# One gathered block's weighted sum of rows moved from VectorE to TensorE, by diagonal matmuls, in a hybrid decoder block

## The chip, the cores and the metric

The kernel runs on one core of one Trainium2 chip. The metric is the device time of one execution in microseconds (us); smaller is better. TensorE (PE) multiplies matrices, VectorE (DVE) and ScalarE (ACT) work element by element, GpSimd (POOL) here issues the gathers and does some subtractions, SyncE (SP) issues the other DMAs.

## The reference

A decoder block on 1024 tokens of width 1024: windowed attention and a gated short convolution (the mixer), a layer norm, and then a channel mixer in which each token uses 128 of 16384 experts (8 heads with 16 each), and a second layer norm. The part that matters here:

```python
def chunk(args):
    xc, ec, gc = args                       # tokens, their 128 experts, their gates
    u = jnp.take(u_experts, ec, axis=0)
    a = jax.nn.gelu(jnp.einsum('tkd,td->tk', u, xc), approximate=False)
    vv = jnp.take(v_experts, ec, axis=0)
    return jnp.einsum('tk,tkd->td', gc * a, vv)
...
ff = peer_ffn(h, ...)
h = layer_norm(DN_ALPHA * h + ff, ln2_g[l], ln2_b[l])
```

All inputs are float32.

## The kernel before

The 1024 tokens are eight blocks of 128. Four of them (`DENSE`, blocks 2 to 5) go through all 16384 experts with dense matmuls, where a token's gate is zero for an expert that it didn't choose. The other four (`ROWS`, blocks 0, 1, 6, 7) gather their experts' rows. So TensorE and VectorE share the channel mixer.

Stage 1 (`s1`) does the mixer for groups of two blocks in order (`GROUPS`), then `normed`, then `keys_of` (16 projections "h" with float32 matmuls at L370, and the top-16 of the scores on VectorE, L196 to L200). `chosen` turns these into expert numbers (`idx`) and gates; for the dense blocks `gates_of_all` writes the gate of every expert: per eight tokens VectorE makes three masks `o1`, `oh`, `ol` (L256, L261; they share four buffers), TensorE multiplies them in two groups of four tokens (eight float16 matmuls each, L267 and L268, into the one PSUM buffer `pk`), ScalarE takes each group out with two copies into the halves of `st` (L271), and after 32 tokens two DMAs of 1 MB store both halves in memory (L275). `st` has two buffers, so the first copy of the next 32 tokens waits until these have landed.

Stage 2 (`s2`) is the dense part: `up` (L684) and `down` (L716), 6144 matmuls of 512 columns.

Beside all of this run the 1024 steps of the gathered blocks, from a generator `gathered(tb)`, in the order block 0, 1, 6, 7. For each block, 128 "u" steps: POOL gathers 128 rows of `u` (one per token, 512 KB together) with an indirect DMA (L148), and VectorE multiplies them with the tokens and sums (L150). Then 128 "v" steps: POOL gathers 128 rows of `v` (L160), and VectorE adds them, weighted per token by a column of `a`, to a PSUM accumulator (L162). Then `second_norm`. All rows, the token blocks and the norm's parameters share five buffers (tag `t4k`). POOL's queue holds the gathers in the order of the steps, and each waits for the buffer that the step five before it leaves.

Steps are drawn by `advance_rows` (beside each projection of stage 1) and by `advance` (in stage 2, spread over nine tenths of its units). A scheduler then sets the order on each engine by its own estimate of times, so steps of the first units of stage 2 stand in stage 1's last part. Each engine works in its order.

Of the kernel before, what the change touches and what calls it, by code (L numbers as in the profile page):

```python
# [13 lines left out]
F32 = mybir.dt.float32  # L14
# [5 lines left out]
AF = mybir.ActivationFunctionType  # L20
ALU = mybir.AluOpType
# [4 lines left out]
P = 128  # L26
T = 1024
D = 1024
# [7 lines left out]
ALPHA = 2.0 ** 0.25  # L36
# [5 lines left out]
GROUPS = [[0, 1], [2, 3], [4, 5], [6, 7]]  # L42
DENSE = [2, 3, 4, 5]
ROWS = [0, 1, 6, 7]
# [10 lines left out]
NGATHER = 5  # L55
# [22 lines left out]
def block_kernel(ctx: ExitStack, tc: tile.TileContext, d, out):  # L78
    nc = tc.nc
    act = nc.scalar.activation  # L80
    V = nc.vector
    G = nc.gpsimd
# [5 lines left out]
    h1d = dram.tile([NB, P, D], F32, name="h1d")  # L88
# [4 lines left out]
    ident = const.tile([P, P], F32, name="ident")  # L93
    make_identity(nc, ident)

    idx, gw, e12 = {}, {}, {}

    def layer_norm(o, src, par, small, sums=None):

        s = small.tile([P, 8], F32, name="lnst", bufs=2)  # L100
        junk = small.tile([P, D], F16, name="junk")
        if sums is None:
            act(junk, src, AF.Copy, accum_out=s[:, 0:1])
        else:
            V.tensor_reduce(s[:, 0:1], sums, axis=AX.X, op=ALU.add)  # L105
        V.tensor_scalar(s[:, 1:2], s[:, 0:1], -1.0 / D, None, op0=ALU.mult)  # L106
        act(junk, src, AF.Square, bias=s[:, 1:2], accum_out=s[:, 2:3])  # L107
        V.tensor_scalar(s[:, 3:4], s[:, 2:3], 1.0 / D, EPS, op0=ALU.mult, op1=ALU.add)  # L108
        act(s[:, 4:5], s[:, 3:4], AF.Sqrt)  # L109
        V.reciprocal(s[:, 5:6], s[:, 4:5])  # L110

        V.tensor_tensor(s[:, 6:7], s[:, 5:6], s[:, 5:6], op=ALU.mult)  # L112
        V.tensor_tensor(s[:, 6:7], s[:, 6:7], s[:, 3:4], op=ALU.mult)  # L113
        V.tensor_scalar(s[:, 6:7], s[:, 6:7], -0.5, 1.5, op0=ALU.mult, op1=ALU.add)  # L114
        V.tensor_tensor(s[:, 5:6], s[:, 5:6], s[:, 6:7], op=ALU.mult)  # L115
        V.scalar_tensor_tensor(o, src, s[:, 1:2], par[0], op0=ALU.add, op1=ALU.mult)  # L116
        V.scalar_tensor_tensor(o, o, s[:, 5:6], par[1], op0=ALU.mult, op1=ALU.add)  # L117
# [8 lines left out]
    gp = ctx.enter_context(tc.tile_pool(name="gp", bufs=1, reuse_waits="tile"))  # L126
    pg = ctx.enter_context(tc.tile_pool(name="pg", bufs=1, space=PS, reuse_waits="tile"))

    def second_norm(tb, src):
        par = []  # L130
        for i in (2, 3):
            p = gp.tile([P, D], F32, name="ln2", tag="t4k", bufs=NGATHER)
            G.dma_start(p, ln2d[:, i:i + 1].to_broadcast([P, 1, D]).rearrange("p a e -> p (a e)"))
            par.append(p)
        o = gp.tile([P, D], F32, name="o", tag="t4k", bufs=NGATHER)
        layer_norm(o, src, par, gp)
        G.dma_start(out[tb * P:(tb + 1) * P], o)

    def gathered(tb):
        g = gw[tb].rearrange("p h k -> p (h k)")  # L140
        h1 = gp.tile([P, D], F32, name="h1", tag="t4k", bufs=NGATHER)
        G.dma_start(h1, h1d[tb])
        h1p = pg.tile([P, D], F32, name="pg")
        act(h1p, h1, AF.Copy)
        a = gp.tile([P, P], F32, name="a", bufs=2)
        for k in range(P):
            row = gp.tile([P, D], F32, name="row", tag="t4k", bufs=NGATHER)
            G.indirect_dma_start(out=row, out_offset=None, in_=d["u"],  # L148
                                 in_offset=bass.IndirectOffsetOnAxis(ap=idx[tb][:, k:k + 1], axis=0))
            V.scalar_tensor_tensor(row, row, 1.0, h1p, op0=ALU.mult, op1=ALU.mult, accum_out=a[:, k:k + 1])  # L150
            yield True
        act(a, a, AF.Gelu)
        V.tensor_tensor(a, a, g, op=ALU.mult)
        acc = pg.tile([P, D], F32, name="pg")
        h1 = gp.tile([P, D], F32, name="h1", tag="t4k", bufs=NGATHER)
        G.dma_start(h1, h1d[tb])
        act(acc, h1, AF.Copy, scale=ALPHA)
        for k in range(P):
            row = gp.tile([P, D], F32, name="row", tag="t4k", bufs=NGATHER)
            G.indirect_dma_start(out=row, out_offset=None, in_=d["v"],  # L160
                                 in_offset=bass.IndirectOffsetOnAxis(ap=idx[tb][:, k:k + 1], axis=0))
            V.scalar_tensor_tensor(acc, row, a[:, k:k + 1], acc, op0=ALU.mult, op1=ALU.add)  # L162
            yield True
        second_norm(tb, acc)

    def all_gathered():
        for tb in ROWS:
            while tb not in idx:
                yield False
            yield from gathered(tb)  # L170

    steps = all_gathered()
    done = 0

    def step():
        nonlocal done
        done += bool(next(steps, False))
# [5 lines left out]
    with ExitStack() as s1:  # L183
# [304 lines left out]
        def conv(gi, c, x, y):  # L488

            blocks, nb, n, t0 = spans(gi)  # L490
            pc = project(10 + c, x, n)
            gc = p2.tile([P, NM], F32, name="cT", bufs=2)
            act(gc[:, :n], pc[:, :n], AF.Identity, bias=bias[:, 10 + c:11 + c])
            px = project(14 + c, x, n)
            u = pa.tile([P, NM + 2], F32, name="u")
            V.tensor_copy(u[:, 0:2], utail[:, c])
            V.scalar_tensor_tensor(u[:, 2:n + 2], px[:, :n], bias[:, 14 + c:15 + c], gc[:, :n],
                                   op0=ALU.add, op1=ALU.mult)
            V.tensor_copy(utail[:, c], u[:, n:n + 2])
            cv = pa.tile([P, NM], F32, name="cv")  # L500
            act(cv[:, :n], u[:, 0:n], AF.Copy, scale=convw[:, c, 0:1])
            for t in (1, 2):
                V.scalar_tensor_tensor(cv[:, :n], u[:, t:t + n], convw[:, c, t:t + 1], cv[:, :n],
                                       op0=ALU.mult, op1=ALU.add)
            pg = project(6 + c, x, n)
            V.scalar_tensor_tensor(y[:, 4 + c, :n], pg[:, :n], bias[:, 6 + c:7 + c], cv[:, :n],
                                   op0=ALU.add, op1=ALU.mult)

        def mixed(gi, y):

            blocks, nb, n, t0 = spans(gi)
            r = p1.tile([P, nb, D], F32, name="r", tag="r")
            rsum = p1.tile([P, nb, 8], F32, name="rsum", bufs=2)
            with tc.issue_after(loads[-1].ins):
                nc.sync.dma_start(r, d["x"][t0:t0 + n].rearrange("(b p) e -> p b e", p=P))
            for c in range(8):
                ps = project(18 + c, y, n)
                mT = p2.tile([P, NM], F32, name="cT", bufs=2)
                act(mT[:, :n], ps[:, :n], AF.Identity, bias=bias[:, 18 + c:19 + c])
                tp = pt.tile([P, 4, P], F32, name="tp")  # L520
                for b in range(nb):
                    nc.tensor.transpose(tp[:, b], mT[:, b * P:(b + 1) * P], ident)
                for b in range(nb):
                    rc = r[:, b, c * P:(c + 1) * P]
                    V.scalar_tensor_tensor(rc, rc, ALPHA, tp[:, b], op0=ALU.mult, op1=ALU.add,
                                           accum_out=rsum[:, b, c:c + 1])
            return r, rsum
# [41 lines left out]
        def chosen(gi):  # L569
            for tb in sorted(GROUPS[gi], key=lambda t: t in ROWS):  # L570
                yield from product_keys(tb, *best[tb])
# [34 lines left out]
        row = gb.tile([P, P], F16, name="keyrow")  # L606
# [13 lines left out]
        for scale, bits, count in ((4096.0, 7, 4), (1.0, 11, 3)):  # L620
# [3 lines left out]
            for c in _pieces(full, bits, count):  # L624
# [5 lines left out]
                        op0=ALU.is_gt, op1=ALU.mult)  # L630
# [7 lines left out]
        for gi, blocks in enumerate(GROUPS):  # L638
            x, qkv = xin
            y = p2.tile([P, NJ, NM], F32, name="y", tag="T", bufs=4)  # L640
            for b in range(2):
                a = scores(gi, b, qkv)
                conv(gi, 2 * b, x, y)
                values(b, y, *a)
                conv(gi, 2 * b + 1, x, y)
            r, rsum = mixed(gi, y)
            if gi + 1 < len(GROUPS):
                xin = rows_in(gi + 1)
            h = normed(gi, r, rsum)
            keys_of(gi, h)  # L650
            for _ in side:
                pass
            side = chosen(gi)


    with ExitStack() as s2:
# [112 lines left out]
        for i in (2, 3):  # L769
            p = gp.tile([P, D], F32, name="ln2", tag="t4k", bufs=NGATHER)  # L770
# [44 lines left out]
```

## Time and profile before

| | us |
|---|---|
| median of 3 runs | 2745.84 (2740.81 to 2745.84) |
| the profiled execution's own time | 2743.4 |
| its span in the profile | 2741.6 |
| TensorE busy in the span | 2290.9 (84%) |
| VectorE busy | 2303.3 (84%) |
| ScalarE busy | 798.1 (29%) |
| GpSimd busy | 1415.2 (52%) |

A busy TensorE is not TensorE at its peak: matmuls overlap in the records. "PEclk" is the share of TensorE's full clock (2.4 GHz) that was granted; 0.5 is its lower level (1.2 GHz). "DMA" is the mean busy share of the 16 DMA engines. Shares over the whole span are means of stages with different limits, so the stages are read apart.

### The profile page before, as it was taken

Reading aid. Unit: us, or ns where it says so; the run is one execution under the profiler, and the core shown is the slowest. Engines: PE = TensorE matmul, PEld = TensorE weight load, DVE = VectorE, ACT = ScalarE, POOL = GpSimd, SP = SyncE. Lnnn points to the kernel's source line nnn. Section 1 sums busy time; section 2 is a strip of 40 time slices with the busy share of each in tenths; the row PEclk is TensorE's granted clock in tenths of the full one; section 3 lists DMA queues with packets and bytes.
Section 4 is the critical chain, followed back from the end, with each engine's and each line's share of the span. In section 5 each row is a group of like instructions: output and inputs, shape, how many; then the busy total and the mean of one; then the engine's idle time right before and its main releaser. Section 6 shows DMA issues by size and latency. Waiting matters only on the chain. (4 is left out here: it accounts for less than half of the span.)

```text
span 2741.6 us, 33269 instructions
## 1 busy us (share of the span) xinstructions
PE 2290.9 (84%) x11032; PEld 1917.8 (70%) x11032; DVE 2303.3 (84%) x4956; ACT 798.1 (29%) x1307; POOL 1415.2 (52%) x1233
## 2 busy tenths in 40 slices
PE   8999699789887622219999999999999999999940
PEld 7888587678766522218888888888888888888830
DVE  2158889999999999978888888888888888888897
ACT  2123122242443323224232322323232332323201
POOL 1000533443353344436667676666767666666753
PEclk9899799799977755559999999999999999999975
DMA  6355999899979788899999999999999999999987
GB/s 203 99 155 175 347 376 332 311 336 354 337 286 337 253 317 293 309 337 322 343 337 340 336 352 350 341 351 335 342 354 334 347 344 346 339 342 353 335 314 263
DMA packets 293900, 862.21 MB, mean 314 GB/s; under 512 B 25824, under 2 KB 97760, under 8 KB 289504
## 3 DMA queue, kind: packets, MB, share of 16 engines
q0 software_dynamic: 150480, 548.47, 54.5%
q1 hardware_dynamic: 143248, 311.62, 33.1%
q8 instruction: 87, 1.43, 0.2%
q14 instruction: 85, 0.70, 0.1%
HBM read 815.95 MB, written 44.04 MB: 314 GB/s over the span
## 5 line engine op out<-in xcount | busy, mean ns | idle before, releaser
L148 POOL DMA_INDIRECT row<-in_u,ix x512 | 532.9, 1041 | 586.7 <-DVE row L150 242.9
L160 POOL DMA_INDIRECT row<-in_v,ix x512 | 554.8, 1084 | 474.4 <-DVE pg L162 229.9
L162 DVE SCALAR_TENSOR_TENSOR pg<-row,a,pg 128x1024 f32<-128x1024 f32 x512 | 656.4, 1282 | 33.8 <-DMA row<-in_v,ix 27.8
L684 PE MATMUL pd<-hT,uh 128*128 128x512 f32 x2048 | 635.8, 390 | 42.8 <-ACT uh L120 42.8
L150 DVE SCALAR_TENSOR_TENSOR row<-row,pg 128x1024 f32<-128x1024 f32 x512 | 611.7, 1212 | 45.4 <-DMA row<-in_u,ix 44.8
L684 PEld LDWEIGHTS pd<-hT,uh 128*128 128x128 f32 x2048 | 385.4, 188 | 123.0 <-ACT uh L120 43.0
L716 PE MATMUL pd<-Wl,vh 128*128 128x512 f32 (+1 forms) x1056 | 402.3, 383 | 0.0
L684 PE MATMUL pd<-hT,ul 128*128 128x512 f32 x1024 | 399.3, 390 | 0.0
L716 PE MATMUL pd<-Wh,vh 128*128 128x512 f32 (+1 forms) x1056 | 397.4, 383 | 0.2 <-ACT Wh L120 0.2
L716 PE MATMUL pd<-Wh,vl 128*128 128x512 f32 (+1 forms) x1056 | 392.1, 383 | 0.3 <-POOL vl L121 0.3
L121 POOL TENSOR_TENSOR vl<-vraw,vh 128x1024 fp32r<-128x1024 f32 x128 | 309.4, 2417 | 72.7 <-ACT vh L120 68.6
L267 PE MATMUL pk<-o,oh 128*128 128x128 f16 x512 | 109.2, 277 | 208.2 <-DVE oh L261 131.3
L370 PE MATMUL mm<-x,raw 128*128 128x256 f32 x1152 | 269.2, 386 | 13.1 <-DMA x<-in_xT 7.7
L120 ACT ACTIVATE vh<-vraw 128x1024 fp32r<-128x1024 f32 x128 | 135.9, 1062 | 455.7 <-PE pd L716 302.1
L722 DVE TENSOR_TENSOR accT<-accT,pd 128x512 f32<-128x512 f32 (+1 forms) x256 | 169.4, 667 | 109.8 <-PE pd L716 97.8
L370 PEld LDWEIGHTS mm<-x,raw 128*128 128x128 f32 x1152 | 215.8, 193 | 45.2 <-issue 8.1
L370 PE MATMUL mm<-h,raw 128*128 128x256 f32 x1024 | 238.1, 385 | 1.5 <-ACT h L539 1.0
L716 PEld LDWEIGHTS pd<-Wh,vl 128*128 128x128 f32 x1056 | 198.4, 188 | 39.3 <-POOL vl L121 0.7
L716 PEld LDWEIGHTS pd<-Wl,vh 128*128 128x128 f32 x1056 | 198.5, 188 | 38.9 <-DVE Wl L121 0.2
L716 PEld LDWEIGHTS pd<-Wh,vh 128*128 128x128 f32 x1056 | 198.0, 188 | 39.2 <-ACT Wh L120 0.4
L121 DVE TENSOR_TENSOR ul<-uraw,uh 128x1024 fp32r<-128x1024 f32 x128 | 159.7, 1248 | 76.1 <-ACT uh L120 70.8
L684 PEld LDWEIGHTS pd<-hT,ul 128*128 128x128 f32 x1024 | 192.8, 188 | 40.9 <-DVE ul L121 0.8
(211 smaller groups left out, 2756.0 us busy)
## 6 DMA issues: line engine op xcount, KB each, us to landing
raw<-in_wall SPq DMA_DIRECT2D x168, 512.0 KB
uraw<-in_uT SPq DMA_DIRECT2D x128, 512.0 KB
vraw<-in_vL SPq DMA_DIRECT2D x128, 512.0 KB
gd<-st SPq DMA_DIRECT2D x32, 1024.0 KB
gq<-gd SPq DMA_DIRECT2D x32, 1024.0 KB
row<-in_u,ix POOLq DMA_INDIRECT x512
row<-in_v,ix POOLq DMA_INDIRECT x512
x<-in_xT SPq DMA_DIRECT2D x16, 256.0 KB
```

Source lines behind the costliest of these rows:

```text
L120: act(dh, src, AF.Copy)
L121: eng.tensor_tensor(dl, src, dh.bitcast(F32), op=ALU.subtract)
L148: G.indirect_dma_start(out=row, out_offset=None, in_=d["u"], in_offset=bass.IndirectOffsetOnAxis(ap=idx[tb][:, k:k + 1], axis=0))
L150: V.scalar_tensor_tensor(row, row, 1.0, h1p, op0=ALU.mult, op1=ALU.mult, accum_out=a[:, k:k + 1])
L160: G.indirect_dma_start(out=row, out_offset=None, in_=d["v"], in_offset=bass.IndirectOffsetOnAxis(ap=idx[tb][:, k:k + 1], axis=0))
L162: V.scalar_tensor_tensor(acc, row, a[:, k:k + 1], acc, op0=ALU.mult, op1=ALU.add)
L267: nc.tensor.matmul(ps[:, t], oh[:, :, t2 + t], o1[:, t2 + t], start=True, stop=False)
L370: nc.tensor.matmul(ps[:, :n], w[:, j], mov[:, j, :n], start=(j == 0), stop=(j == NJ - 1))
L684: nc.tensor.matmul(ps, w[:, j], hT[z][:, j], start=(j == 0 and k == 0), stop=(j == NJ - 1 and k == 2))
L716: nc.tensor.matmul(ps, vv[:, j % 2, k], w[:, t0:t0 + n], start=(k == 0 and p == 0), stop=(k == QUAD - 1 and p == 2))
L722: V.tensor_tensor(o, o, ps, op=ALU.add)
```

## The change

The generator is taken apart: `weights_of(tb)` does a block's u steps, `summed(tb, a)` its v steps as before. Now blocks 0 and 1 do their u steps first, then block 0 does its v steps by `summed_on_pe`, then block 1 by `summed`; blocks 6 and 7 follow as before. In `summed_on_pe` ScalarE makes a 128x128 diagonal matrix `dg` with the column of `a` on its diagonal (two buffers), and TensorE multiplies it with the gathered rows, in two float32 matmuls of 512 columns that add up in PSUM over all 128 rows. The last hunk draws steps where the rest of `side` (the generator of `chosen`) is used up in the last group.

```diff
+    def weights_of(tb):
+
+        while tb not in idx:
+            yield False
         h1p = pg.tile([P, D], F32, name="pg")
-        act(h1p, h1, AF.Copy)
+        act(h1p, own(tb), AF.Copy)
         a = gp.tile([P, P], F32, name="a", bufs=2)
         for k in range(P):
...
+            row = rows_of(tb, "u", k)
             V.scalar_tensor_tensor(row, row, 1.0, h1p, op0=ALU.mult, op1=ALU.mult, accum_out=a[:, k:k + 1])
             yield True
         act(a, a, AF.Gelu)
...
+    def summed(tb, a):
+
         acc = pg.tile([P, D], F32, name="pg")
...
+        act(acc, own(tb), AF.Copy, scale=ALPHA)
         for k in range(P):
...
-            V.scalar_tensor_tensor(acc, row, a[:, k:k + 1], acc, op0=ALU.mult, op1=ALU.add)
+            V.scalar_tensor_tensor(acc, rows_of(tb, "v", k), a[:, k:k + 1], acc, op0=ALU.mult, op1=ALU.add)
             yield True
         second_norm(tb, acc)
 
+    def summed_on_pe(tb, a):
+
+        acc = pg.tile([P, D], F32, name="pg")
+        for k in range(P):
+            row = rows_of(tb, "v", k)
+            dg = gp.tile([P, P], F32, name="dg", bufs=2)
+            act(dg, ident, AF.Copy, scale=a[:, k:k + 1])
+            for z in range(0, D, 512):
+                nc.tensor.matmul(acc[:, z:z + 512], dg, row[:, z:z + 512], start=(k == 0), stop=(k == P - 1))
+            yield True
+        V.scalar_tensor_tensor(acc, own(tb), ALPHA, acc, op0=ALU.mult, op1=ALU.add)
+        second_norm(tb, acc)
+
     def all_gathered():
...
+        a0 = yield from weights_of(ROWS[0])
+        a1 = yield from weights_of(ROWS[1])
+        yield from summed_on_pe(ROWS[0], a0)
+        yield from summed(ROWS[1], a1)
+        for tb in ROWS[2:]:
+            a = yield from weights_of(tb)
+            yield from summed(tb, a)
...
             keys_of(gi, h)
             for _ in side:
-                pass
+                if gi == len(GROUPS) - 1 and done < 3 * P:
+                    step()
             side = chosen(gi)
```

Two places in the order of the built programs show where the new instructions stand. The first is TensorE's order in stage 1 after the last projection, in the gates of the last two dense blocks. Before, one group of eight matmuls (with `oh` and `ol` in turn) follows the other; here is the end of one eight-token set and the start of the next:

```order
L268 LDWEIGHTS ol
L268 MATMUL pk<-o_7424,ol 128x128
L267 LDWEIGHTS oh
L267 MATMUL pk<-o_7483,oh 128x128
L268 LDWEIGHTS ol
L268 MATMUL pk<-o_7483,ol 128x128
```

Now, at the same kind of place (line numbers are those of the changed kernel; L182 is the new matmul, L291 and L292 are the former L267 and L268):

```order
L292 LDWEIGHTS ol
L292 MATMUL pk<-o_6938,ol 128x128
L182 MATMUL pg<-row,dg 128x512 x4
L291 LDWEIGHTS oh
L291 MATMUL pk<-o_6993,oh 128x128
L292 LDWEIGHTS ol
L292 MATMUL pk<-o_6993,ol 128x128
```

So two gathered rows (four matmuls) now stand between almost every two groups of gate matmuls; behind the last score matmul of `keys_of` there are 250 of the 256 new matmuls and all 64 gate groups of these two blocks.

The second place is ScalarE's order where one set of 32 tokens ends and the next begins, with what each instruction waits for (DMAHW is the store of the former 32 tokens). Before, the copies follow each other:

```order
L271 ACTIVATE st<-pk 128x4x64 [waits PE_49]
L271 ACTIVATE st<-pk 128x4x64
L271 ACTIVATE st<-pk 128x4x64 [waits DMAHW3_49,PE_49,Activation_49]
L271 ACTIVATE st<-pk 128x4x64 [waits DMAHW4_49,Activation_49]
L271 ACTIVATE st<-pk 128x4x64 [waits PE_49]
```

Now (L180 makes a diagonal, L295 is the former L271):

```order
L295 ACTIVATE st<-pk 128x4x64 [waits PE_49]
L295 ACTIVATE st<-pk 128x4x64
L180 ACTIVATE dg<-ident,a 128x128 [waits PE_49,Activation_49] x2
L295 ACTIVATE st<-pk 128x4x64 [waits DMAHW5_49,PE_49,Activation_49]
L180 ACTIVATE dg<-ident,a 128x128 [waits PE_49,Activation_49] x2
L295 ACTIVATE st<-pk 128x4x64 [waits DMAHW6_49]
L180 ACTIVATE dg<-ident,a 128x128 [waits PE_49,Activation_49]
```

The diagonals stand in the same queue as the copies that wait for the stores, two of them ahead of the first such copy and two between the copies.

## Rows read from the trace of the kernel before

**Rows 1.** The page: the span in 40 equal slices (busy tenths, granted clock).

```profile
PE   8999699789887622219999999999999999999940
DVE  2158889999999999978888888888888888888897
PEclk9899799799977755559999999999999999999975
```

**Rows 2.** Busy time by stretch: A:B, length, then PE, PEld, DVE, ACT, POOL (instructions), PEclk, DMA share, GB/s.

```profile
548.00:847.00 299.00, 251.98 (x1457) 214.53 (x1456) 294.97 (x869) 118.12 (x246) 122.98 (x105) 0.87 0.89 325
847.00:920.00 73.00, 71.07 (x390) 61.81 (x388) 72.50 (x229) 23.04 (x46) 27.12 (x27) 0.95 0.92 341
949.00:1189.00 240.00, 66.49 (x456) 51.05 (x456) 227.70 (x604) 70.09 (x126) 113.92 (x113) 0.50 0.85 305
1189.00:1231.00 42.00, 0.34 (x1) 0.34 (x2) 24.56 (x44) 7.79 (x8) 14.14 (x15) 0.50 1.04 380
1231.00:2631.00 1400.00, 1399.47 (x6259) 1161.58 (x6259) 1191.27 (x1506) 432.01 (x539) 944.73 (x720) 1.00 0.95 341
2631.00:2715.00 84.00, 1.65 (x16) 1.41 (x13) 71.22 (x57) 0.00 (x0) 48.93 (x53) 0.53 0.95 340
```

**Rows 3.** Costliest groups of the page: the steps on VectorE, float32 matmuls and their loads.

```profile
L162 DVE SCALAR_TENSOR_TENSOR pg<-row,a,pg 128x1024 f32<-128x1024 f32 x512 | 656.4, 1282 | 33.8 <-DMA row<-in_v,ix 27.8
L150 DVE SCALAR_TENSOR_TENSOR row<-row,pg 128x1024 f32<-128x1024 f32 x512 | 611.7, 1212 | 45.4 <-DMA row<-in_u,ix 44.8
...
L370 PE MATMUL mm<-x,raw 128*128 128x256 f32 x1152 | 269.2, 386 | 13.1 <-DMA x<-in_xT 7.7
...
L370 PEld LDWEIGHTS mm<-x,raw 128*128 128x128 f32 x1152 | 215.8, 193 | 45.2 <-issue 8.1
```

**Rows 4.** Timeline of VectorE, two places: start, us, instruction.

```profile
1145.83 1.21 DVE L150 SCALAR_TENSOR_TENSOR row<-row,pg 128x1024 f32<-128x1024 f32 x1
...
1146.97 1.21 DVE L150 SCALAR_TENSOR_TENSOR row<-row,pg 128x1024 f32<-128x1024 f32 x1
...
605.26 1.27 DVE L162 SCALAR_TENSOR_TENSOR pg<-row,a,pg 128x1024 f32<-128x1024 f32 x1
606.45 0.21 DVE L205 TENSOR_TENSOR x<-x 128x128 f16<-128x128 f16 x1
```

**Rows 5.** Timeline of TensorE within the last projections.

```profile
888.44 5.35 PE L370 MATMUL mm<-h,raw 128*128 128x256 f32 x24
...
898.50 0.22 PE L267 MATMUL pk<-o,oh 128*128 128x128 f16 x1
...
898.99 1.08 PE L370 MATMUL mm<-h,raw 128*128 128x256 f32 x4
```

**Rows 6.** Timeline of ScalarE where one set of 32 tokens ends (in brackets: idle before, releaser).

```profile
1083.08 1.05 ACT L271 ACTIVATE st<-pk 128x256 f32<-128x256 f32 x2 [4.83 <-PE pk L268]
...
1085.23 1.06 ACT L271 ACTIVATE st<-pk 128x256 f32<-128x256 f32 x2 [1.10 <-issue]
...
1092.62 0.61 ACT L271 ACTIVATE st<-pk 128x256 f32<-128x256 f32 x1 [6.33 <-DMA gd<-st]
1096.15 0.60 ACT L271 ACTIVATE st<-pk 128x256 f32<-128x256 f32 x1 [2.92 <-DMA gd<-st]
```

**Rows 7.** Busy time by stretch, as in rows 2: all seven such ends, and their sum.

```profile
1048.00:1062.30 14.30, 2.67 (x12) 1.69 (x13) 14.30 (x41) 2.72 (x5) 6.21 (x6) 0.50 0.98 365
1086.30:1096.80 10.50, 1.29 (x8) 1.01 (x9) 8.79 (x23) 1.21 (x2) 4.13 (x4) 0.50 0.99 385
...
sum 80.30, PE 11.68 PEld 8.59 DVE 71.27 ACT 9.71 POOL 34.19; mean PE 1.67 PEld 1.23 DVE 10.18 ACT 1.39 POOL 4.88
```

**Rows 8.** ScalarE on a 128x128 tile: ns min/median/max, first and last start.

```profile
L152 ACT ACTIVATE a<-a x4: 309/310/310, 555.2 to 2461.8; 128x128 f32<-128x128 f32 x4
```

**Rows 9.** Busy time by stretch, as in rows 2: a pause of TensorE and what follows.

```profile
588.00:595.00 7.00, 1.84 (x19) 1.47 (x19) 7.00 (x22) 2.69 (x6) 4.72 (x3) 0.71 0.90 312
595.00:602.00 7.00, 5.11 (x32) 4.38 (x32) 7.00 (x10) 3.65 (x7) 1.14 (x1) 0.56 0.64 197
```

More of the change, by code (lines that the diff above doesn't have):

```diff
@@ L137, in second_norm, with rows_of, own @@
         G.dma_start(out[tb * P:(tb + 1) * P], o)
-    def gathered(tb):
-        g = gw[tb].rearrange("p h k -> p (h k)")
+    def rows_of(tb, table, k):
+        row = gp.tile([P, D], F32, name="row", tag="t4k", bufs=NGATHER)
+        G.indirect_dma_start(out=row, out_offset=None, in_=d[table],
+                             in_offset=bass.IndirectOffsetOnAxis(ap=idx[tb][:, k:k + 1], axis=0))
+        return row
+    def own(tb):
         h1 = gp.tile([P, D], F32, name="h1", tag="t4k", bufs=NGATHER)
         G.dma_start(h1, h1d[tb])
+        return h1
+    def weights_of(tb):
+        while tb not in idx:
+            yield False
         h1p = pg.tile([P, D], F32, name="pg")
-        act(h1p, h1, AF.Copy)
+        act(h1p, own(tb), AF.Copy)
         a = gp.tile([P, P], F32, name="a", bufs=2)
         for k in range(P):
-            row = gp.tile([P, D], F32, name="row", tag="t4k", bufs=NGATHER)
-            G.indirect_dma_start(out=row, out_offset=None, in_=d["u"],
-                                 in_offset=bass.IndirectOffsetOnAxis(ap=idx[tb][:, k:k + 1], axis=0))
+            row = rows_of(tb, "u", k)
             V.scalar_tensor_tensor(row, row, 1.0, h1p, op0=ALU.mult, op1=ALU.mult, accum_out=a[:, k:k + 1])
@@ L152, in gathered @@
         act(a, a, AF.Gelu)
-        V.tensor_tensor(a, a, g, op=ALU.mult)
+        V.tensor_tensor(a, a, gw[tb].rearrange("p h k -> p (h k)"), op=ALU.mult)
+        return a
+    def summed(tb, a):
         acc = pg.tile([P, D], F32, name="pg")
-        h1 = gp.tile([P, D], F32, name="h1", tag="t4k", bufs=NGATHER)
-        G.dma_start(h1, h1d[tb])
-        act(acc, h1, AF.Copy, scale=ALPHA)
+        act(acc, own(tb), AF.Copy, scale=ALPHA)
         for k in range(P):
-            row = gp.tile([P, D], F32, name="row", tag="t4k", bufs=NGATHER)
-            G.indirect_dma_start(out=row, out_offset=None, in_=d["v"],
-                                 in_offset=bass.IndirectOffsetOnAxis(ap=idx[tb][:, k:k + 1], axis=0))
-            V.scalar_tensor_tensor(acc, row, a[:, k:k + 1], acc, op0=ALU.mult, op1=ALU.add)
+            V.scalar_tensor_tensor(acc, rows_of(tb, "v", k), a[:, k:k + 1], acc, op0=ALU.mult, op1=ALU.add)
             yield True
         second_norm(tb, acc)
-    def all_gathered():
[L167 to L170, printed above, removed]
+    def summed_on_pe(tb, a):
[9 more added lines that the diff above has]
+        second_norm(tb, acc)
+    def all_gathered():
+        a0 = yield from weights_of(ROWS[0])
[5 more added lines that the diff above has]
+            yield from summed(tb, a)
     steps = all_gathered()
```

## The prediction

> **What bounds the kernel now.** I read the slices first [rows 1]: TensorE is nearly always busy but for a hole near the end of stage 1 and a hole at the end, and in the first hole VectorE is full. The stretches [rows 2] give each part its own limit. From 548 to 847 us VectorE is busy in 295 of 299 us: it bounds. From 847 to 920 the last 16 projections run and TensorE (71.1 of 73) and VectorE (72.5) are both full. From 920 to 1189 the gates of blocks 4 and 5 are made; in the 240 us from 949 VectorE is busy 228, TensorE 66 at the granted clock 0.50, DMA 0.85. From 1189 to 1231 both wait for loads of stage 2 (DMA 1.04 of its engines). From 1231 to 2631 TensorE is busy 1399 of 1400 us at clock 1.00 and VectorE 1191: stage 2 is TensorE's, and a later start of it is a later end. From 2631 to 2715 only v steps run, on VectorE and DMA; 27 us of norms and stores follow.
>
> So VectorE's relief can pay between 548 and 1189 and in the last 84 us, and TensorE's new work must fit into stage 1's hole.
>
> **The change, part by part.** Sums are made against the profiled execution, 2743.4 us (0.1% under the median of 2745.84).
>
> *Number of steps.* The last hunk does nothing: 84 items of `side` are left when the last group starts, and its 36 projections draw 84 (two each, and a third in 12 of them). What moves the steps is the scheduler. In the order of the built programs VectorE has, ahead of stage 2's first gate product, 389 steps before (256 u, 133 v), and now 256 u and 15 v, with TensorE's 128 beside them: 399. Between there and the last of these products 570 steps stand in both, so 55 v steps are left for the tail instead of 65. The tail's 56 steps took 84 us [rows 2], 1.5 us each: **-15 us**.
>
> *Up to the last projections: u steps instead of v steps.* Where the residual rows of the last group are done, 128 u and 90 v stood before, now 233 u; at its first top-8, 128 u and 107 v, now 256 u. Means of 1212 and 1282 ns [rows 3] overstate both, as records overlap: a u step takes 1.14 us from start to next start, a v step 1.19 [rows 4]. That is 233 x 1.14 - (146 + 107) = +13 us at the one place, and 292 - (146 + 127) = +19 us at the other. VectorE bounds there, so I take **+15 us** for the start of the projections: 847 becomes 862.
>
> *The projections* were full on TensorE already and have no u or v step on VectorE now, so their 73 us stay. They end at 935.
>
> *The gates with the new matmuls.* A float32 matmul is recorded as two: 72 projections of x with 8 matmuls each are 1152 records [rows 3]. 24 records of 256 columns take 5.35 us with 0.39 for the last one's own length, so 4.96 / 23 = 0.216 us each at the full clock [rows 5]. At 512 columns I take twice that, 0.43; a gathered row (two matmuls, four records) is 1.72 us, at half the clock 3.44. Eight gate matmuls take 0.49 us at full clock [rows 5]. After the last score matmul TensorE now has 125 rows and 64 gate groups: 125 x 1.72 + 64 x 0.49 = 215 + 31 = 246 us. The bound from below is that alone.
>
> The weight loads are taken as hidden: each of those 24 records has its own load of 0.19 us [rows 3, 5], and 0.216 has no room for it. The Trainium skill (TensorE: Matmul & The Clock Gate, Part 3, The mechanism) says that a load overlaps matmuls in flight only where it goes to other rows of the array; these loads fill all rows, so by it each would stand between two records. By that rule the sum would be an estimated 125 x 4 x 0.19 = 95 us more; the trace does not agree with it.
>
> The stores add gaps. After each 32 tokens ScalarE waits until both have landed: its next two copies came 6.3 us, and then another 2.9, late [rows 6]; the stretch from the last copy to the end of the next pair is 80.3 / 7 = 11.5 us in the mean [rows 7], with DMA at 365 to 385 GB/s, so it won't shrink. Before, VectorE worked on there. Now TensorE has the rows: it ends two rows about 2.1 us into the stretch (a copy pair ends some 1.3 us after its group), the next group at 2.6, two more rows, whose diagonals stand ahead of the wait, at 6.0. The third's diagonal comes behind the first copy, at 6.3 + 0.6 + 0.3 [rows 6, 8]: a gap of 1.2 us; it ends at 9.0, and the next group needs the second copy out of `pk`, at 11.5: 2.5 us. So 3.7 us for each of seven ends: 26 us. (Nothing, if the stores land sooner; 5.5 each, 39, if the third row waits for the second copy too.) What is late next is the row buffers, then the gathers.
>
> The clock: a pause of TensorE before 595 (1.8 of 7 us busy) is followed by a stretch at 0.56 [rows 9]. Each gap could cost nothing, or 3.5 us, if 7 us behind it run at half the clock as there. I take half of that, 1.7 each: 12 us.
>
> The last 32 tokens have five rows only; there the copies set the pace, 2.15 us per group [rows 6]: 8 x 2.15 - 5 x 1.72 - 8 x 0.49 = 5 us more, and with block 0's norm on the same queues 8. In all 246 + 26 + 12 + 8 = 292 us, where 920 to 1189 was 269: **+23 us**.
>
> *What is at nothing.* The diagonals: 128 x 0.31 us on ScalarE [rows 8], busy 70 of 240 us [rows 2]. Block 0's norm, its loads and store move from before 949 to the passage into stage 2; hidden behind stage 2's loads, at most 2 MB at 380 GB/s, 5 us. In stage 2 nothing is bound by VectorE.
>
> Sum: 15 + 23 - 15 = +23 us, **2766 us**.
>
> **Rivals.** *Faster or equal: TensorE hides the gaps.* If gaps and clock together cost less than 15 us instead of 38, the sum is zero or below; with none of them, +13 and the tail it is 13 + (254 - 269) - 15 = -17, 2726 us. For it: VectorE, the former bound, loses more than 110 steps of 1.14 us in this stretch, and TensorE had 73 us at 0.95 with hardly a gap before. Against it: the diagonals wait in ScalarE's queue behind copies that wait for DMA, and the rows fill TensorE's time already. Faster 0.21, within 0.2% 0.12.
>
> *Gathers late.* TensorE takes its rows in order, and a late one holds the gates too. The stretch moves 125 rows of 0.52 MB and 17 MB of stores, 82 MB in 292 us, 283 GB/s; before it was 305, and the ends have reached 385. Five buffers at 2.2 us a row leave 11 us for a round. But at each end a row could come 5 us late: 35 us more, 2801. Chance 0.10.
>
> *The clock stays at half.* 125 x 3.44 + 64 x 0.98 = 493 us instead of 246, 3013. At 0.50 TensorE was busy 28% of the time [rows 2]; now it would be full, and full stretches have 0.95 and more. Partly so, 0.05. *The rule on weight loads*, 2861: 0.02.
>
> **How the numbers follow.** The forecast, 2752 to 2795, has 0.50. Below: 2726 with all gaps hidden. Above: gaps of 39, clock of 25, +19, and 5 for the passage give 19 + (246 + 39 + 25 + 8 - 269) - 15 + 5 = +58, 2801, as the late gathers do. Some 0.1 lies past 2805 and 0.1 under 2726. So 2726 to 2805. A measurement of this kernel can tell 0.2%, 5.5 us, from no change: faster 0.21, same 0.12, slower 0.67.
>
> **What would show it.** The first "h" projection after 855 and the last gate copy near 1220 to 1230 instead of 1188; stage 2's first matmul some 40 us later, and stage 2 of 1400 us again; L182 with 512 records, 0.43 us apart within a row; TensorE over 80% busy in the gates at a clock over 0.8, with VectorE far from full; idle time of TensorE that ends with a diagonal or a copy, at each store; 46 v steps after TensorE's end instead of 56. I am wrong if the gates end before 1190 (gaps hidden), if rows wait for gathers or the clock for hundreds of us, or if stage 2 changes its length.

## The result, and the profile after

The changed kernel takes 2767.54 us in the median of four runs (2761.45 to 2772.54), the kernel before 2745.84 (2740.81 to 2747.0, four runs): a ratio of 1.0082 [1.0056, 1.0107], slower by 0.8%. The forecast was 2766. The profiled execution of the changed kernel is its fastest, 2761.45 us with a span of 2759.6, so against before's span of 2741.6 the traces have to explain +18 us, and the medians +22.

The page of the changed kernel, the span in 40 slices; beside [rows 1] the hole of TensorE in slices 14 to 18 is mostly filled, its clock is up there, and VectorE's 9, 9, 9, 9, 7 in these slices have become 8, 4, 4, 2, 3.

```profile
PE   8999699779876999966999999999999999999960
DVE  2158889999999844238888788888888888888898
PEclk9899799789977999987999999999999999999985
```

Busy time by stretch of the changed kernel, columns as in [rows 2]: up to the last projections, the projections, the gates, the passage, stage 2, the tail.

```profile
548.00:847.00 299.00, 243.73 (x1393) 208.30 (x1391) 295.09 (x968) 109.86 (x233) 118.91 (x117) 0.85 0.92 339
862.00:935.00 73.00, 73.00 (x425) 64.50 (x424) 62.80 (x287) 23.88 (x47) 9.07 (x9) 0.98 0.60 211
935.00:1224.00 289.00, 262.75 (x1036) 131.38 (x1034) 122.22 (x403) 130.79 (x278) 126.71 (x128) 0.98 0.83 286
1224.00:1265.00 41.00, 0.00 (x0) 0.00 (x0) 20.09 (x17) 5.96 (x7) 15.48 (x16) 0.50 1.03 369
1265.00:2665.00 1400.00, 1399.34 (x6256) 1161.71 (x6257) 1188.64 (x1506) 432.77 (x541) 926.47 (x720) 1.00 0.95 342
2665.00:2733.00 68.00, 2.01 (x19) 1.77 (x17) 58.71 (x47) 0.00 (x0) 39.84 (x44) 0.54 0.96 345
```

VectorE still bounds until the projections (295 of 299). Then the roles change over: in the gates TensorE is busy 263 of 289 us and VectorE 122, where before VectorE was full and TensorE half empty. Stage 2 is 1400 us as before; the tail has 47 instructions on VectorE where it had 57.

The groups of the gates stretch (instructions and shape | busy, mean ns | idle before, releaser) say who waits for whom now:

```profile
L182 PE MATMUL pg<-row,dg 128*128 128x512 f32 x508 | 236.6, 606 | 14.3 <-ACT dg L180 11.0 <-DMA row<-in_v,ix 3.3
...
L285 DVE TENSOR_TENSOR oh<-da,db 128x1024 f16<-128x1024 f16 x32 | 22.0, 689 | 159.7 <-PE pk L291 159.7
```

VectorE idles 159.7 us for TensorE's gate matmuls (L291), because the 508 records of 127 rows take TensorE 236.6 us. The rows themselves wait 11.0 us for diagonals and only 3.3 for gathers.

A table puts both kernels, and the experiments below, on one scale (us, read from the trace of each kernel; the five parts add up to the span): the start of the last projection; from there to the start of the last gate copy; the passage to stage 2's first matmul; stage 2 to the start of its last matmul; and the tail from there.

| kernel | to last projection | gates | passage | stage 2 | tail | span |
|---|---|---|---|---|---|---|
| before | 919.8 | 268.5 | 42.4 | 1399.9 | 111.0 | 2741.6 |
| after | 934.5 | 289.9 | 41.0 | 1399.6 | 94.6 | 2759.6 |
| order only | 936.9 | 233.4 | 42.3 | 1401.8 | 138.1 | 2752.5 |
| diagonals on VectorE | 936.5 | 300.5 | 43.0 | 1403.8 | 98.3 | 2782.1 |
| three `st` | 933.7 | 254.5 | 40.5 | 1406.2 | 120.6 | 2755.5 |
| half the rows | 937.9 | 245.6 | 45.2 | 1401.5 | 129.8 | 2760.0 |
| float32r rows | 939.6 | 213.9 | 43.7 | 1409.3 | 200.4 | 2806.9 |
| float32r, six buffers | 923.6 | 221.4 | 43.5 | 1399.4 | 104.2 | 2692.1 |
| before, six buffers | 920.1 | 272.7 | 40.1 | 1399.9 | 79.0 | 2711.8 |
| after, six buffers | 927.1 | 294.1 | 48.3 | 1398.4 | 68.4 | 2736.3 |

After against before: +14.7 up to the last projection, +21.4 in the gates, -1.4 in the passage, -0.3 in stage 2, -16.4 in the tail: +18.

### The profile page after: what moved, and what is told of

Same layout as the page of the kernel before. It is cut to its first block, busy times and chain, and to the rows that moved or that the text cites. A ratio compares the mean times of both kernels' runs of the same rounds, so it can differ in the third digit from the quotient of the medians.

```text
span 2759.6 us, 34442 instructions
## 1 busy us (share of the span) xinstructions
PE 2476.9 (90%) x11544; PEld 1992.3 (72%) x11544; DVE 2156.7 (78%) x4829; ACT 842.6 (31%) x1434; POOL 1378.8 (50%) x1233
## 5 line engine op out<-in xcount | busy, mean ns | idle before, releaser
L141 POOL DMA_INDIRECT row<-in_u,ix x512 | 526.0, 1027 | 625.0 <-DVE row L159 234.9
L141 POOL DMA_INDIRECT row<-in_v,ix x512 | 525.9, 1027 | 486.5 <-PE pg L182 199.9
L170 DVE SCALAR_TENSOR_TENSOR pg<-row,a,pg 128x1024 f32<-128x1024 f32 x384 | 493.3, 1285 | 38.4 <-DMA row<-in_v,ix 34.2
L182 PE MATMUL pg<-row,dg 128*128 128x512 f32 x512 | 238.7, 606 | 14.3 <-ACT dg L180 11.0
L394 PEld LDWEIGHTS mm<-x,raw 128*128 128x128 f32 x1152 | 216.3, 193 | 43.5 <-issue 7.9
```

The lines of the kernel that those rows point to most:

```text
L141: G.indirect_dma_start(out=row, out_offset=None, in_=d[table], in_offset=bass.IndirectOffsetOnAxis(ap=idx[tb][:, k:k + 1], axis=0))
L170: V.scalar_tensor_tensor(acc, rows_of(tb, "v", k), a[:, k:k + 1], acc, op0=ALU.mult, op1=ALU.add)
L182: nc.tensor.matmul(acc[:, z:z + 512], dg, row[:, z:z + 512], start=(k == 0), stop=(k == P - 1))
L394: nc.tensor.matmul(ps[:, :n], w[:, j], mov[:, j, :n], start=(j == 0), stop=(j == NJ - 1))
```

## The experiments

The theory, A: the float32 rows make TensorE the bound of the gates, and each row costs it more (some 1.75 us) than VectorE's step cost (1.19). Against it stood that something else sets the end of the gates: the new order of the steps, the pauses at the stores with their clock, or the gathers. The expectations, quoted below, name the theories by letters: A is this one, B says that the new order of the steps alone makes stage 2 late, and C that gathered rows come late.

**Order only.** All u steps of blocks 0 and 1 first, and every v step on VectorE:

```
-        yield from summed_on_pe(ROWS[0], a0)
+        yield from summed(ROWS[0], a0)
```

> The new order of the steps (u of blocks 0 and 1 first) with all v steps left on VectorE, no diagonal matmuls. Theory A (the loss comes from TensorE's new rows in the gates): VectorE bounds the gates again as before; the first last-group projection starts near 864 us as in the changed kernel, the last gate copy near 1190 instead of 1224, stage 2 starts near 1232; the order leaves 82 v steps to the tail instead of 65 (before) or 55 (changed), about 26 us more than before; 2755 to 2775 us in all, but by the tail, not by the gates. Theory B (the new order of the steps alone makes stage 2 late): the last gate copy stays near 1224 here too.

Measured: 2759.77 us, ratio 1.0050 [1.0033, 1.0066]. The last copy starts at 1170.3, before both kernels; the gates take 233 us, 57 less than with the matmuls. Stretches of this kernel (gates, tail):

```profile
937.00:1171.00 234.00, 78.48 (x542) 60.95 (x540) 224.61 (x558) 82.77 (x152) 118.10 (x83) 0.51 0.74 257
...
2614.00:2725.00 111.00, 2.39 (x22) 2.15 (x20) 93.38 (x74) 0.00 (x0) 65.71 (x71) 0.52 0.95 337
```

VectorE is the bound again (225 of 234), with TensorE at clock 0.51. It holds fewer steps: 84 v steps stand in this stretch, 118 u steps stood in before's. They are paid at the end, where 73 steps are left, 1.5 us each, instead of 55. The new order alone costs +17 ahead of the gates, gives 35 in them and loses 27 in the tail. So the longer gates of the changed kernel come from the matmuls and not from the order: A holds, though the gates came out shorter than expected.

The order alone is slower than before, though, by 11 us of span. Of the changed kernel's +18 only some 7 come with the matmuls: 57 us more in the gates, 44 less in the tail, where 45 steps are left instead of 73, and 6 less in the other parts. The two kernels' ratios to before, 1.0050 and 1.0082, have intervals that overlap, so these 7 us are near the edge of what the runs can tell.

**Diagonals on VectorE**, so that they don't wait behind copies in ScalarE's queue:

```
-            act(dg, ident, AF.Copy, scale=a[:, k:k + 1])
+            V.tensor_scalar(dg, ident, a[:, k:k + 1], None, op0=ALU.mult)
```

> The diagonals are made by VectorE instead of ScalarE. Theory A with its second part (the gaps at the stores come from diagonals and copies in ScalarE's queue): the gap before the third row at each of seven stores goes, the one before the copy out of the PSUM buffer stays; TensorE's idle time in the gates falls by 7 to 15 us and the last gate copy comes 5 to 15 us earlier; 2745 to 2765 us. Theory C (gathered rows come late at the stores, since DMA is full there): gaps and time unchanged within 3 us.

Measured: 2784.49 us, ratio 1.0141 [1.0125, 1.0158]: a miss. The gates became longer by 11 us, not shorter. One store end, timeline of TensorE (start, us, instruction, in brackets idle before and releaser), then three stretches across it:

```profile
1019.98 1.96 PE L182 MATMUL pg<-row,dg 128*128 128x512 f32 x4 [0.78 <-DMA row<-in_v,ix]
1024.56 0.27 PE L291 MATMUL pk<-o,oh 128*128 128x128 f16 x1 [2.62 <-ACT st L295]
...
1025.37 3.01 PE L182 MATMUL pg<-row,dg 128*128 128x512 f32 x4
```

```profile
1018.00:1024.50 6.50, 3.16 (x7) 1.01 (x6) 0.57 (x2) 1.20 (x2) 2.57 (x3) 0.97 1.01 415
1024.50:1027.50 3.00, 2.94 (x11) 1.91 (x11) 1.89 (x3) 1.14 (x3) 0.00 (x0) 0.50 0.91 373
1027.50:1058.00 30.50, 29.22 (x115) 14.50 (x115) 9.81 (x24) 6.66 (x13) 14.05 (x15) 1.00 0.77 256
```

The wait for the diagonal did go. But the gate group's wait for a copy out of `pk` (L295) remains, and here it is one pause of 2.6 us, behind which the granted clock is 0.50 for some 3 us: four records take 3.01 us there, 1.96 at the full clock. Six of the sets of 32 tokens end with such a pause, of 2.3 to 2.6 us, and each of these is followed by half the clock; a seventh drop came behind a pause of 1.2 us. TensorE is idle 28 us in the gates instead of 26, and busy 271 instead of 263: seven stretches of 3.4 us at half the clock, where the changed kernel has two, make 5 x 1.7 = 8.5 us. So the wait behind the copies moved and did not shrink, and the clock fell behind it more often.

**Three `st` buffers**, so that the copies wait less for the stores (and one `kd` buffer less, to make room):

```
-                st = [gb.tile([P, NC // 2, TG], F32, name="st", bufs=2) for _ in range(2)]
+                st = [gb.tile([P, NC // 2, TG], F32, name="st", bufs=3) for _ in range(2)]
...
-            kd = pa.tile([P, 2, 2, HD], F32, name="kd", bufs=2)
+            kd = pa.tile([P, 2, 2, HD], F32, name="kd", bufs=1)
```

> Three buffers for the gate copies st instead of two (and one instead of two for a small tile of the attention, to make room). Theory A: the first copy after each 32 tokens no longer waits for a store, the second waits for the store that lands first; TensorE's gaps there fall from some 23 us in all to under 10. The order now leaves 12 rows behind the last gate and 71 v steps to the tail, 24 us more there; 2755 to 2780 us in all, the last gate copy before 1195 instead of 1224. Theory C (late gathers): gaps stay.

Measured: 2756.84 us (eight runs), ratio 1.0036 [1.0025, 1.0047]. Gates, and tail:

```profile
934.00:1189.00 255.00, 238.30 (x963) 121.13 (x962) 110.59 (x375) 119.21 (x251) 113.64 (x115) 0.99 0.84 292
2635.00:2729.00 94.00, 1.91 (x18) 1.67 (x16) 80.18 (x63) 0.00 (x0) 54.92 (x60) 0.53 0.95 338
```

TensorE's idle time in the gates fell from 26 to 17 us, less than hoped, but the gates are 35 us shorter: most of the rest is that 46 records, 11 or 12 rows (20 us), now come behind the last copy, where stage 2's loads hide them (the passage is no longer for it). TensorE is full in what is left (238 of 255), as A has it. The tail takes 26 us of the gain back, and a stage 2 that is longer by 7 takes more.

**Half the rows** on TensorE, the other 64 as v steps on VectorE:

```
-        for k in range(P):
+        half = P // 2
+        for k in range(half):
...
-                ... start=(k == 0), stop=(k == P - 1))
+                ... start=(k == 0), stop=(k == half - 1))
+            yield True
+        for k in range(half, P):
+            V.scalar_tensor_tensor(acc, rows_of(tb, "v", k), a[:, k:k + 1], acc, op0=ALU.mult, op1=ALU.add)
             yield True
```

> Half of block 0's v rows by diagonal matmuls (64), the other 64 on VectorE onto the same sum. Theory A (TensorE's 1.72 us a row bound the gates): TensorE has 61 rows and 64 groups there, 136 us, and no longer bounds; VectorE has some 185; the gates end where their own copies and stores end, 8 x (8 x 2.15) + 7 x 11.5 = 218 to 245 us after the last projection, near 1155 to 1185 instead of 1224. The order leaves 77 v steps to the tail instead of 55, 33 us more; 2725 to 2755 us in all. Theory C (gathers bound): the gates take 290 us again, 2775 to 2800 in all.

Measured: 2762.24 us, ratio 1.0061 [1.0044, 1.0078]. The gates stretch, and its two parts, with the rows on TensorE and behind them:

```profile
938.00:1184.00 246.00, 166.89 (x782) 94.74 (x780) 168.93 (x439) 103.20 (x208) 126.03 (x106) 0.78 0.83 288
...
938.00:1075.00 137.00, 127.96 (x506) 63.97 (x504) 64.53 (x272) 61.42 (x132) 64.21 (x63) 1.00 0.84 289
1075.00:1184.00 109.00, 38.93 (x276) 30.77 (x276) 104.40 (x168) 41.78 (x77) 61.83 (x44) 0.51 0.82 287
```

The gates are 44 us shorter than with all rows, and end at 1184, within what A gave for them. But not for A's reason, that the copies and stores set their end: over the whole stretch TensorE and VectorE have 167 and 169 us of 246, yet they take turns. While the rows last, TensorE is full (128 of 137) and VectorE half empty; then VectorE is full (104 of 109) and TensorE at half the clock. Rows and v steps drawn in turn, so that both engines work at once, were not run. The total is 7 us above A's range, since the tail holds 68 steps and lasts 130 us, 35 more. A shorter stretch that makes fewer steps pays later.

**Float32r rows.** Block 0's rows and diagonals are read as float32r, for which TensorE's trace has one record per matmul instead of two:

```
-            row = rows_of(tb, "v", k)
-            dg = gp.tile([P, P], F32, name="dg", bufs=2)
+            row = gp.tile([P, D], F32R, name="row", tag="t4k", bufs=NGATHER)
+            G.indirect_dma_start(out=row, out_offset=None, in_=d["v"].bitcast(F32R), ...)
+            dg = gp.tile([P, P], F32R, name="dg", bufs=2)
```

> The changed kernel with block 0's v rows and diagonals as float32r, one record per 512 columns as in stage 2's matmuls instead of two slower ones (the products of this block are rounded more coarsely; the rest is unchanged). Theory A (TensorE's time per row bounds the gates): a row takes 0.45 us instead of 1.75, TensorE has some 90 us of work there, and the gates end where their copies and stores end, 215 to 250 us after the last projection, the last gate copy near 1155 to 1185 instead of 1224. Theory C (the gathers bound, 125 rows in 290 us): the gates take 280 us or more again. The order leaves 123 v steps behind the last gate product of stage 2 instead of 55, some 100 us more in the tail, so 2790 to 2830 us in all by A and 2850 to 2880 by C.

Measured: 2807.06 us, ratio 1.0222 [1.0188, 1.0257]. The gates stretch and the tail; then one row, and in the gates what the rows (L184) and the gate groups (L293) waited for:

```profile
940.00:1154.00 214.00, 125.93 (x739) 83.54 (x738) 118.18 (x395) 113.35 (x252) 111.31 (x105) 0.80 0.95 325
2606.00:2780.00 174.00, 2.53 (x23) 2.29 (x21) 145.63 (x115) 0.00 (x0) 103.18 (x111) 0.52 0.94 338
```

```profile
992.03 0.71 PE L184 MATMUL pg<-row,dg 128*128 128x512 f32 x2
...
L184 PE MATMUL pg<-row,dg 128*128 128x512 f32 x211 | 87.2, 507 | 28.2 <-DMA row<-in_v,ix 25.0 <-ACT dg L182 3.0
L293 PE MATMUL pk<-o,oh 128*128 128x128 f16 x256 | 47.3, 250 | 58.9 <-ACT st L297 56.5 <-DVE oh L287 1.5 <-DVE ol L287 0.9
```

A row by itself takes 0.71 us here from its first start to its last end, so TensorE's work is more than the 90 us expected, but far less than 263: it is busy 126 of 214 us, and the gates are 76 us shorter. The price of a float32 row was the bound of the gates in the changed kernel, as A says. (The order of this kernel also leaves 22 fewer rows in the stretch, 105 where the changed kernel has 127; at 1.75 us each they are 38 us, so as much as half of the 76 could be their place and not their price.) TensorE's waits are now those for the copies, 56.5 us by the gate groups, and for the gathers, 25 us by the rows, which waited 3.3 in the changed kernel. But the order of this kernel leaves 113 steps for the tail, and it is the slowest of all, as A said of the total too.

**Six row buffers**, `NGATHER = 5` made 6, in three kernels: the float32r one, before, and after.

> As e5 with six row buffers instead of five, with which the order leaves 69 v steps instead of 123. Theory A: the gates end near 1155 to 1185, stage 2 starts 35 to 65 us before that of the changed kernel, and the tail is some 20 us longer: 2715 to 2750 us. Theory C: gates as in the changed kernel, 2770 to 2800.

> The kernel before with six row buffers instead of five; the order leaves 49 v steps instead of 65 behind the last gate product of stage 2, and puts 14 more u steps ahead of the last gate. If the steps' place decides (theory A): the tail 24 us shorter, the gates up to 16 us longer, as VectorE bounds them: 2725 to 2745 us. If the gathers bound the gates and the tail (theory C), the sixth buffer lets more of them fly, and both become shorter: under 2720.

> The changed kernel with six row buffers; the order leaves 42 v steps instead of 55, the rows on TensorE stay where they are. Theory A: the gates take 285 to 295 us again, with TensorE as busy as in the changed kernel, and the tail is some 20 us shorter: 2740 to 2755 us. Theory C (rows come late on TensorE): the gates become shorter by 15 us or more: under 2735.

Measured: with float32r rows 2694.69 us, ratio 0.9813 [0.9786, 0.9840]; before 2713.61, 0.9879 [0.9854, 0.9903]; after 2732.46, 0.9945 [0.9921, 0.9969] (all three against the kernel before with five). All three are faster than the totals that A gave, and the totals of before and after lie where C had put them (under 2720, under 2735). The gates are as A has them, 273 us in before and 294 in after with six buffers (269 and 290 with five), so the gathers don't set them in either kernel; C's half on the tail came true. First the tail of before with six buffers and its v steps, with what they waited for, below those with five; then gates and tail of the float32r kernel with six:

```profile
2633.00:2685.00 52.00, 1.87 (x18) 1.63 (x15) 50.67 (x41) 0.00 (x0) 33.17 (x37) 0.54 0.99 383
...
L162 DVE SCALAR_TENSOR_TENSOR pg<-row,a,pg 128x1024 f32<-128x1024 f32 x56 | 72.2, 1289 | 12.8 <-DMA row<-in_v,ix 11.1 <-DVE pg L162 0.4
...
L162 DVE SCALAR_TENSOR_TENSOR pg<-row,a,pg 128x1024 f32<-128x1024 f32 x40 | 51.6, 1290 | 1.3
```

```profile
924.00:1146.00 222.00, 132.02 (x755) 88.74 (x754) 119.10 (x398) 116.71 (x262) 119.02 (x114) 0.78 0.99 340
...
2588.00:2666.00 78.00, 1.96 (x18) 1.72 (x17) 75.92 (x63) 0.31 (x1) 51.03 (x56) 0.54 1.00 387
```

The sixth buffer pays in the tail, which I had priced at 1.5 us a step throughout: DMA moves 383 GB/s instead of 340 [rows 2], a step takes 52 / 40 = 1.3 us, and fewer steps are left (39 instead of 55 in before). With five buffers VectorE waited 11 us for gathers there, with six for none: at 1.29 us a step the tail now goes at VectorE's own pace. In the float32r kernel this adds up: the cheap rows keep the gates at 221 us, and the tail goes from 200 to 104. It beats both kernels, and before with six buffers by 19 us; how float32r changes the sums of block 0 was not measured here. With six buffers in both, after is still slower than before, by 2732.46 - 2713.61 = 19 us.

## Why the prediction was right

*The sum.* Forecast +15, +23 and -15, measured from the traces +15 (919.8 to 934.5), +21 (268.5 to 289.9) and -16 (111.0 to 94.6), with -2 for passage and stage 2. Each term has its sign and nearly its size. They don't price the matmuls alone, a split that the prediction did not make: by the kernel with the order alone, the gates' +21 are -35 by the order and +57 by the matmuls, the tail's -16 are +27 and -44.

*u steps instead of v steps.* VectorE is as full as it was between 548 and 847 (295 of 299) and the projections start at 864, where 862 was forecast. In the kernel with the order alone they start at 869, where before has 847, so this belongs to the order and not to the matmuls.

*The projections* nearly kept their length: 864.4 to 934.5, 70 us from the first start to the last where before has 72.5 (847.3 to 919.8), wholly TensorE's (73.0 of 73), with VectorE relieved to 63.

*The gates* came out at 290 for 292, but the pieces were mis-sized, in both directions. TensorE's own work was put at 246 us and is 263. Part of that is the row: records of 512 columns follow each other as here (TensorE of the changed kernel, timeline; between the two rows stands one gate group of eight records):

```profile
994.16 3.65 PE L182 MATMUL pg<-row,dg 128*128 128x512 f32 x8
...
998.15 3.65 PE L182 MATMUL pg<-row,dg 128*128 128x512 f32 x8
```

Eight records take 3.65 us with 0.59 for the last one's own length: 3.06 / 7 = 0.437 us each, 1.75 a row where I took 1.72; and 3.99 - 2 x 1.75 = 0.49 for the gate group, as forecast. With 127 rows in the stretch, where 125 were counted, this is 127 x 1.75 + 64 x 0.49 = 254 us; the clock adds 3.4 and transposes of other stages 3; some 3 us of the 263 stay unplaced.

The pauses were put at 26 + 8 us; TensorE is idle 26 us in all. One end of 32 tokens in the changed kernel, timeline of ScalarE and TensorE:

```profile
1014.10 3.65 PE L182 MATMUL pg<-row,dg 128*128 128x512 f32 x8
1018.78 0.60 ACT L295 ACTIVATE st<-pk 128x256 f32<-128x256 f32 x1 [4.52 <-DMA gd<-st]
1019.18 0.65 ACT L180 ACTIVATE dg<-ident,a 128x128 f32<-128x128 f32 x2
1019.60 1.98 PE L182 MATMUL pg<-row,dg 128*128 128x512 f32 x4 [1.86 <-ACT dg L180]
1022.40 0.60 ACT L295 ACTIVATE st<-pk 128x256 f32<-128x256 f32 x1 [2.56 <-DMA gd<-st]
1023.05 0.22 PE L291 MATMUL pk<-o,oh 128*128 128x128 f16 x1 [1.46 <-ACT st L295]
```

It is the forecast chain: a copy waits for the store, the diagonal stands behind the copy, the row behind the diagonal (1.9 us, forecast 1.2; a diagonal takes 0.40 us where 0.31 was taken); the second copy waits again, and the next group for it (1.5 us, forecast 2.5). Of the seven ends one differs: there the rows waited for gathers, 3.3 us in all.

The clock was put at 12 us and cost 3.4, which the 263 hold already. It fell at two of the ends only, to half for 3.4 us each, behind pauses of 2.1 and 2.2 us. One of them, a row at half the clock, 3.18 us where 1.98 stands above, and the stretch at 0.50:

```profile
1134.04 3.18 PE L182 MATMUL pg<-row,dg 128*128 128x512 f32 x4 [2.14 <-ACT dg L180]
...
1134.70:1138.10 3.40, 3.18 (x11) 1.25 (x10) 0.00 (x0) 0.93 (x2) 0.61 (x1) 0.50 1.02 414
```

So the two mis-sized terms are the clock (12 us, measured 3.4) and TensorE's work (246, measured 260 without the clock's part); with the pauses at 26 instead of 34 they cancel, and the gates' total was met better than its pieces, which is luck.

*The weight loads* are hidden, as taken: every record has a load of about 0.19 us [rows 3], and records of 512 columns start 0.437 us apart, twice the 0.216 of 256 columns, so a fixed 0.19 us is no part of either. The Trainium skill (TensorE: Matmul & The Clock Gate, Part 3, The mechanism) says in its list that loads overlap matmuls in flight only where they go to other rows of the array; by that the stretch would be some 95 us longer, and this trace does not agree. (The same section also names a background weight buffer, into which a load may go ahead of matmuls in flight; the prediction took the list alone.) Why a float32 row is so dear is told by the Trainium skill (FP8 and Floating Point Precision, TensorE Precision Notes): true float32 goes through the array in four passes. With a column per cycle from matmul to matmul (the Trainium skill, TensorE: Matmul & The Clock Gate, Part 2, Step-by-step: what each phase is for) that is an estimated 4 x 512 / 2.4 GHz = 0.85 us; the trace agrees, with two records of 0.437, 0.87 us, for a matmul.

*The tail.* 45 v steps were left for 55, and 16.4 us less: the 1.5 us a step and the count from the order both held.

*The rivals.* "TensorE hides the gaps" falls: pauses and clock cost 26 + 3 us, and even with three `st` buffers, 17 us idle and the gates at 254, the tail took the gain back. "Gathers late" falls (3.3 us in the gates, at one end of seven), and so does "the clock stays at half" (0.98).

*The last hunk* was taken to do nothing. It was not run by itself, so that rests on the order of the instructions alone.

*What stays open.* How many steps each order leaves for the tail was counted, not explained: the float32r kernel has 113 there with five buffers and 58 with six, and why the order puts so many more there with five is not shown. Nor is what decides whether the clock falls behind a pause (last section).

## What to carry to other kernels

Work moved from a full engine to a half-empty one pays only if its price on the new engine fits into the idle time: here a step of 1.19 us on VectorE became a row of 1.75 us on TensorE, 127 of them were too many for TensorE's hole beside the gates, and the bound went with the work. Price such a move in the stage where it lands, with the operand type's own record spacing, and count where the displaced steps come out: a stretch that makes fewer background steps only sends them to the tail. Measure the new order without the moved work, too: here it was 11 of the 18 us. Then try the cheapest lever of the tail (one more row buffer) on both kernels, as it was worth more here than the change itself.

## What the runs showed of the hardware

The length of one pause did not decide whether the granted clock fell. The changed kernel's pauses of 1.9 and 1.5 us at a store's end, with a row between them, left it at 1.00, and with the diagonals on VectorE a single pause of 2.3 to 2.6 us was followed by 0.50 at all six ends that have one. That looks as if one pause cost more than two. But in the kernel with three `st` buffers a single pause of 3.3 us left the clock at 1.00, and one of 1.9 us was followed by 0.50 (timeline of TensorE, and the stretch behind each pause):

```profile
963.03 0.22 PE L291 MATMUL pk<-o,oh 128*128 128x128 f16 x1 [3.28 <-ACT st L295]
...
963.00:967.00 4.00, 3.66 (x16) 1.94 (x16) 3.34 (x14) 1.90 (x5) 1.18 (x1) 1.00 0.98 399
...
1103.61 0.22 PE L291 MATMUL pk<-o,oh 128*128 128x128 f16 x1 [1.87 <-ACT st L295]
...
1104.80:1108.20 3.40, 3.40 (x12) 1.75 (x11) 1.34 (x3) 1.12 (x4) 0.77 (x1) 0.50 1.02 417
```

So what these runs show is the price of such a fall, some 1.7 us of TensorE's time where the half clock lasts 3.4 us, and not what brings it about.

The gathers' rate grew with the buffers in flight: with nothing but v steps running, five buffers of 0.52 MB moved 337 to 345 GB/s, six 379 to 387. With six VectorE no longer waited for them, so a limit of the gathers themselves is not shown.
